# Recurrence scores level by level for a pair of head groups, with the projections' matmuls between the levels; six weight splits behind the norm chain; attention's first loads in another order

## The chip, the cores and the metric

The kernel runs on one core of one Trainium2 chip. The metric is the device time of one execution in microseconds (us). Engines are named as in the profile: PE is TensorE's matmul stream, PEld its weight loads, DVE is VectorE, ACT is ScalarE, SP issues the loads from HBM.

## What is computed

A two-layer network over 256 tokens of width 1024: a gated linear recurrence (HGRN2), a feed-forward block (FFN), sparse attention (NSA) with its shared keys and values, and a second FFN, each behind an RMS norm whose shift, scale and gate come from a conditioning vector c. The change touches the recurrence most:

```python
q, f, i, g = jnp.split(h @ w_in, ...)          # 8 heads, 128 keys and 128 values each
q = silu(q); log_f = log_sigmoid(f); k = -expm1(log_f)
# in chunks of 64 tokens, G = cumsum(log_f):
attn = einsum('bhtk,bhsk,bhtsk->bhts', q_, k_, decay)   # decay = exp(G_t - G_s), s <= t
o = attn @ v_ + (q_ * exp(G)) @ state
o = rms_norm(o, out_norm) * silu(g)
return o.reshape(B, S, HGRN_D_VAL) @ w_out
```

## The kernel before

The model's matrices arrive by DMA in tiles `raw` of 128 x 2048 floats. `process` (line 302) splits each half of such a tile into a high part `wh` (a cast on ACT, line 321) and a rest `wl` (a subtraction on DVE, line 325), and a product of the projections is three matmuls, wh by the high part of the activations, wh by their rest, wl by the high part (lines 529 to 531; for the values 972 to 974). DMA slots are few, so the next `raw` is issued when an earlier tile has been read for the last time. The conditioning is worked out by matmuls on the same PE (`adapsg`, `adapsss`, line 425, with transposes `adat`), sprinkled in by a table.

The recurrence handles the 8 heads as four groups i = 0 to 3 of two heads, and two groups make a pair. It does not run a scan. For every group it builds the 256 x 256 decayed score matrix from blocks by halving: `hgrn_decays` (line 994) holds running decays in `rf`, and for each level, with blocks of 1, 2, 4, 8, 16 and 32 tokens and more, writes a scaled copy of queries and keys, `X` (ACT, line 1023; DVE lines 1026 and 1028 carry `rf` to the next level). `hgrn_scores` (line 1033) then has PE multiply them. For each of four (head, token half) corners, `head_scores` issues 24 tiny matmuls into the tile `psl` (32-column diagonal blocks, line 1076, and five levels of 16 columns, line 1082) and 4 into `psu` (lines 1088, 1092); `psx` (line 1049) are the two large off-diagonal blocks. DVE masks `psl` into `ab` and then `A` (lines 1051 to 1062), ACT copies `psu` and `psx` in. `hgrn_values` multiplies A by the values v (`hgpv`, lines 1108 to 1110), normalises (`o`, line 1129), and transposes back (`hgt`, line 1132). The gate product g and the output projection `hgo` with its residual add `x` (line 794) follow.

The order of all this is the list ORDER["hgrn"], one token a step: D decays, i and g the value and gate products of a group, S a group's scores, V values, G gating, o output projection. A "+" puts a step's matmuls into a queue `between` instead, from which `hgrn_scores` draws `fill` steps of three matmuls after each corner (S0/4 draws four). S1 has no fill: its four corners, 96 tiny matmuls, follow each other. Every matmul on float32 data shows in the trace as two records.

`stat_end` (line 707) is the end of an RMS norm: `ms` on PE, a chain of small DVE operations from `nv` by three Newton steps (lines 488 to 493) to `dg`, and `rb` on PE (line 722), which spreads the result. On DVE's queue other work may stand between the links of this chain. ORDER["nsa"] and ORDER["hada"] place the attention's products and the conditioning in the same manner; PE, DVE and ACT each run their queue in program order.

Of the kernel before, what the change touches and what calls it, by code (L numbers as in the profile page):

```python
# [21 lines left out]
P = 128  # L22
# [8 lines left out]
XBUFS = 14  # L31
XMOD, XOFF = 5, 9
WIDE = (1,)
PTS = 3
# [20 lines left out]
def _ada_g(l):  # L55
# [9 lines left out]
        "D0 k i0 g0 S1 i1 +g1 S0/4 x c1 V0 D1 i2 i3 G0 +g2 +g3 +o0 S2/5 S3/5 V1 x H o1 G1 o2 o3"  # L65
# [4 lines left out]
        "c0 q0 c1 K G q1 n0 x0 s0 w0 q2 s1 q3 w1 s2 v0 v1 n1 s3 s4 a v2 v3 a a a x1 s5 a a s6 v4 v5 s7 a v6 a a "  # L70
        "a a v7 a"
# [128 lines left out]
class K:  # L200
# [101 lines left out]
    def process(self):  # L302
# [9 lines left out]
        if kind in ("lin", "half"):  # L312
            ws = []
            for h in range(1 if kind == "half" else 2):
# [10 lines left out]
                nc.vector.tensor_tensor(wl, u, wh.bitcast(F32), op=ALU.subtract)  # L325
# [88 lines left out]
    def ada_pe(self, kind, l, i, t):  # L414
# [19 lines left out]
        pt = self.m_tile([P, 4, P], "adat")  # L434
# [272 lines left out]
    def stat_end(self, ps=None):  # L707
# [11 lines left out]
        for tt in range(2):  # L719
            nc.vector.tensor_scalar_mul(dg[:, tt], self.c("ident"), r[:, tt:tt + 1])  # L720
# [93 lines left out]
    def hgrn(self):  # L814
# [3 lines left out]
        with self.tc.tile_pool(name="hg", bufs=1) as gp, self.tc.tile_pool(name="hg2", bufs=2) as g2:  # L818
# [19 lines left out]
            q = gp.tile([P, 8, S], F32, name="q")  # L838
# [8 lines left out]
            for i in range(4):  # L847
                self.act(q[:, 2 * i:2 * i + 2], pq[i], AF.Silu)
# [75 lines left out]
            Xs = {}  # L924
            for t in ORDER["hgrn"]:
# [3 lines left out]
                elif t[0] == "D":  # L929
                    Xs.update(self.hgrn_decays(logs if n == 0 else self.hgrn_logs({m: pf[m] for m in (2, 3)}, g2), q, g2))  # L930
                elif t[0] == "S":
                    As[n] = self.hgrn_scores(Xs.pop(n), q[:, 2 * n:2 * n + 2], g2, n, between, int(t[3:] or 0))
                elif t[0] == "+":
                    between = chain(between, {"g": gate_steps, "o": out_steps, "i": value_steps}[t[1]](int(t[2])))
# [11 lines left out]
                elif t[0] == "c":  # L946
                    nc.scalar.copy(graw[:, n], gin[n])
                elif t[0] == "V":
                    self.hgrn_values((2 * n, 2 * n + 1), As, v[n], g2, q)
# [44 lines left out]
    def hgrn_decays(self, logs, qs, g2):  # L994
# [16 lines left out]
        for i, rf in rfs.items():  # L1011
            nc.vector.tensor_tensor(rf[:, 0].rearrange("p (h s) -> p h s", h=2), rf[:, 2].rearrange("p (h s) -> p h s", h=2),
                                    qs[:, 2 * i:2 * i + 2], op=ALU.mult)
            nc.vector.tensor_copy(Xs[i][8], rf[:, 1].rearrange("p (h s) -> p h s", h=2))
        for l, b in enumerate(LEVELS):
            n = W // (2 * b)
            for i, rf in rfs.items():
                X = new(i, l)
                if b == 1:
                    odd = [[2, S]]  # L1020
                    nc.scalar.copy(ap(X, 1, *odd), ap(rf, 1, *odd))
                else:
                    last = nc.scalar.copy(ap(X, 0, [b, 2], [2 * b, n], [1, b]), ap(rf, W, [b - W, 2], [2 * b, n], [1, b]))  # L1023
# [9 lines left out]
    def hgrn_scores(self, X, q, g2, i, between, fill):  # L1033
# [3 lines left out]

        psl = self.m_tile([P, 4, 112], f"psl{i}")
        psu = self.m_tile([P, 4, P], f"psu{i}")
        psx = self.m_tile([P, 2, P], f"psx{i}")  # L1040
        for h in range(2):
            for tt in range(2):
                with self.tc.issue_after(prev.ins) if prev else ExitStack():
                    last = self.head_scores(psl, psu, X, q, h, tt)
# [4 lines left out]
            nc.tensor.matmul(psx[:, h], lhsT=X[7][:, h, 0:P], rhs=X[7][:, h, P:2 * P], start=True, stop=True)  # L1049
        ab = g2.tile([P, 4, 32], F32, tag="ab", name=f"ab{i}")  # L1050
        nc.vector.tensor_tensor(ab, psl[:, :, 0:32], self.c("m_d")[:, None, :].to_broadcast([P, 4, 32]), op=ALU.mult)
        ml = self.c("m_l").rearrange("p (l j) -> p l j", l=5)
        for l, b in enumerate(LOW):
# [3 lines left out]
            src = psl[:, :, 32 + 16 * l:48 + 16 * l].rearrange("p a (n b) -> p a n b", b=b)  # L1057
# [11 lines left out]
    def head_scores(self, psl, psu, X, q, h, tt):  # L1069

        nc = self.nc
        ht = h * 2 + tt
        base = tt * P
        for j in range(4):
            s = slice(base + 32 * j, base + 32 * j + 32)
            nc.tensor.matmul(psl[32 * j:32 * j + 32, ht, 0:32], lhsT=X[8][:, h, s], rhs=q[:, h, s],
                             start=True, stop=True, tile_position=(0, 32 * j))
        for l, b in enumerate(LOW):
            for j in range(4):
                s = slice(base + 32 * j, base + 32 * j + 32)  # L1080
# [10 lines left out]
        for j in (64, 0):  # L1091
            last = nc.tensor.matmul(u[j:j + 32, j + 32:j + 64], lhsT=X[5][:, h, base + j:base + j + 32],
                             rhs=X[5][:, h, base + j + 32:base + j + 64], start=True, stop=True,
                             tile_position=(0, j))
        return last

    def hgrn_values(self, ns, As, v, g2, q):
# [19 lines left out]
        else:  # L1117
# [8 lines left out]
            nc.vector.scalar_tensor_tensor(r, t, 1.5, r, op0=ALU.add, op1=ALU.mult)  # L1126
        for a, i in enumerate(ns):
# [540 lines left out]
```

## Time and profile before

| | |
|---|---|
| time, median of 3 runs | 734.29 us (733.88 to 738.5) |
| the profiled execution | 736.01 us, of which the span on the core is 734.2 us |
| TensorE clock granted, mean over the span | 0.998 |
| PE busy | 712.4 us (97%) |
| DVE busy | 580.3 us (79%) |
| ACT busy | 433.6 us (59%) |
| chain that ended last | PE 81%, ACT 7%, DVE 5%, DMA 4%, issue 1% |

The stages on PE's clock: conditioning and the input projections up to 72 us, the recurrence to 192 us, the first FFN to 365 us, keys and values and attention to 555 us, the second FFN to the end. A PE record in the trace lasts longer than its place in the stream, since matmuls are pipelined; the distance between two starts is what one costs.

### The profile page before, as it was taken

How to read it: one execution, taken by the hardware profiler on the slowest of the kernel's cores; microseconds unless marked ns; L12 is line 12 of the kernel's file. 1: busy time of each engine (PE TensorE's matmuls, PEld its weight loads, DVE VectorE, ACT ScalarE, POOL GpSimd, SP SyncE). 2: the span in 40 equal slices, each digit the busy share in tenths (PEclk: the TensorE clock that was granted, in tenths of full speed). 3: DMA queues.
4: the chain of work that ended last, by engine and by line, in shares of the span. 5: the costliest groups of instructions: out<-in, count | busy, mean ns of one | idle time of the engine just before them, and what ended most of it. 6: DMA issues, size and time to landing. Idle time of an engine off the chain costs nothing.

```text
span 734.2 us, 14785 instructions
## 1 busy us (share of the span) xinstructions
PE 712.4 (97%) x5949; PEld 626.6 (85%) x5949; DVE 580.3 (79%) x1177; ACT 433.6 (59%) x849; POOL 0.4 (0%) x5
## 2 busy tenths in 40 slices
PE   7999899999999999999999999999999999999997
PEld 4998688789999999988898897555899888888886
DVE  6997877469999889989589888678689778677651
ACT  5669689347635444534469777558666565655330
POOL 0000000000000000000000000000000000000000
PEclk9999999999999999999999999999999999999999
DMA  8899873823669897988555541654654557556610
GB/s 349 323 370 370 295 285 127 320 81 149 246 232 401 296 363 284 344 314 298 224 191 208 226 170 58 229 205 169 238 192 174 207 203 278 188 214 236 247 69 22
DMA packets 27159, 172.49 MB, mean 235 GB/s; under 512 B 2897, under 2 KB 4305, under 8 KB 7250
## 3 DMA queue, kind: packets, MB, share of 16 engines
q1 hardware_dynamic: 26656, 170.80, 62.7%
q8 instruction: 47, 0.77, 0.4%
q10 hardware_dynamic: 434, 0.74, 0.3%
q14 instruction: 22, 0.18, 0.1%
HBM read 170.48 MB, written 1.05 MB: 234 GB/s over the span
## 4 chain that ended last, share of the span: by engine, by line
PE 81%; ACT 7%; DVE 5%; DMA 4%; issue 1%; SPq 0%; ACTq 0%
PE ffo L541 11%; PE ff L530 6%; PE ff L529 6%; PE ff L531 6%; PE ffo L542 6%; PE ff L541 5%; DMA raw<-in_w 3%; PE po L1546 3%; PE ff L542 2%; PE adapsss L425 2%; ACT wh L321 2%; PE ptt L1529 2%; PE s L1489 2%; DVE wl L325 1%; PE nso L529 1%
## 5 line engine op out<-in xcount | busy, mean ns | idle before, releaser
L321 ACT CAST wh<-raw 128x1024 fp32r<-128x1024 f32 x199 | 207.4, 1048 | 170.2 <-PE ffo L541 48.6
L325 DVE TENSOR_TENSOR wl<-raw,wh 128x1024 fp32r<-128x1024 f32 x199 | 242.0, 1221 | 68.8 <-ACT wh L321 68.3
L541 PE MATMUL ffo<-g,wh 128*128 128x512 f32 x352 | 123.6, 394 | 0.0
L542 PE MATMUL ffo<-g,wl 128*128 128x256 f32 x352 | 99.1, 282 | 0.0
L531 PE MATMUL ff<-hh,wl 128*128 128x256 f32 (+1 forms) x352 | 99.1, 282 | 0.0
L530 PE MATMUL ff<-hl,wh 128*128 128x256 f32 (+1 forms) x352 | 98.8, 282 | 0.0
L529 PE MATMUL ff<-hh,wh 128*128 128x256 f32 (+1 forms) x352 | 98.6, 282 | 0.0
L541 PEld LDWEIGHTS ffo<-g,wh 128*128 128x128 f32 x352 | 66.1, 188 | 15.4
L387 DVE CUSTOM_DVE_ANT_0 junk<-raw,crep 128x1024 f32<-128x1024 f32 x64 | 77.9, 1218 | 1.8 <-DMA raw<-in_w 1.6
L531 PEld LDWEIGHTS ff<-hh,wl 128*128 128x128 f32 x352 | 66.5, 189 | 0.0
L530 PEld LDWEIGHTS ff<-hl,wh 128*128 128x128 f32 x352 | 66.3, 189 | 0.1
L529 PEld LDWEIGHTS ff<-hh,wh 128*128 128x128 f32 x352 | 66.1, 189 | 0.2 <-ACT hh L731 0.2
L542 PEld LDWEIGHTS ffo<-g,wl 128*128 128x128 f32 x352 | 66.1, 188 | 0.0
L541 PE MATMUL ff<-h,wh 128*128 128x512 f32 x152 | 54.0, 394 | 0.0
L542 PE MATMUL ff<-h,wl 128*128 128x256 f32 x152 | 42.6, 281 | 0.0
L541 PEld LDWEIGHTS ff<-h,wh 128*128 128x128 f32 x152 | 28.7, 189 | 6.5
L463 ACT ACTIVATE Pt<-Pt,nm 128x128 f32<-128x128 f32 x64 | 28.2, 442 | 8.1 <-DVE nm L1498 7.9
L794 DVE SCALAR_TENSOR_TENSOR x<-ffo,mod,x 128x256 f32<-128x256 f32 x32 | 15.4, 481 | 19.6 <-PE ffo L542 19.2
L542 PEld LDWEIGHTS ff<-h,wl 128*128 128x128 f32 x152 | 28.6, 188 | 0.0
L524 ACT CAST g<-fg 128x256 fp32r<-128x256 f32 x44 | 17.8, 404 | 14.1 <-DVE fg L1169 13.1
L1494 DVE CUSTOM_DVE_ANT_0 Pt<-s,cst 128x128 f32<-128x128 f32 (+1 forms) x64 | 19.0, 351 | 4.1 <-PE s L1489 4.1
L1026 DVE TENSOR_TENSOR rf<-rf 128x512 f32<-128x512 f32 x28 | 18.3, 685 | 2.8 <-ACT X L1023 1.8
(493 smaller groups left out, 1750.2 us busy)
## 6 DMA issues: line engine op xcount, KB each, us to landing
raw<-in_w SPq DMA_DIRECT2D x153, 1024.0 KB, 5.1
raw<-in_w SPq DMA_DIRECT2D x11, 512.0 KB, 6.6
w1late<-in_w SPq DMA_DIRECT2D x2, 1024.0 KB, 6.5
x<-in_x SPq DMA_DIRECT2D x2, 512.0 KB, 5.3
out<-x SPq DMA_DIRECT2D x8, 128.0 KB, 1.9
cst<-in_cst ACTq DMA_DIRECT2D x1, 558.0 KB
rselr<-in_rsel SPq DMA_DIRECT2D x1, 256.0 KB, 3.5
w<-in_w SPq DMA_DIRECT2D x1, 128.0 KB, 3.4
```

What stands on the lines that cost most here:

```text
L321: r = nc.scalar.copy(wh, u)
L325: nc.vector.tensor_tensor(wl, u, wh.bitcast(F32), op=ALU.subtract)
L387: r = nc.vector.tensor_tensor_reduce(out=junk, in0=t[:, h * D:(h + 1) * D], in1=self.crep, scale=1.0, scalar=0.0, op0=ALU.mult, op1=ALU.ad ...
L463: r = nc.scalar.activation(out, in_, func, **kw)
L529: mm(ps, lhsT=wh, rhs=hh, start=first, stop=False)
L530: mm(ps, lhsT=wh, rhs=hl, start=False, stop=False)
L531: return mm(ps, lhsT=wl, rhs=hh, start=False, stop=last)
L541: mm(ps, lhsT=w[k][0], rhs=b, start=k == 0, stop=False)
L542: mm(ps[:, 0], lhsT=w[k][1], rhs=b[:, 0], start=False, stop=k == n - 1)
L1026: nc.vector.tensor_tensor(fr, fr, ap(rf, 2 * W, [1, 2], [2, n], [0, b]), op=ALU.mult)
L1494: nc.vector.tensor_tensor_reduce(out=Pt[half][:, br, o:o + n], in0=ps[half][:, br], in1=cs[:, S - n:], scale=1.0, scalar=-3e38, op0=ALU.ad ...
L1546: nc.tensor.matmul(po[64 * half:64 * half + 64, t], lhsT=w[:, half], rhs=rhs, start=n == 0, stop=n == len(steps) - 1, tile_position=(0, 64 ...
```

## The change

It does five things.

1. Scores go by pair and by level: for a pair of groups the six levels are run one after the other, each as one slot of 16 matmuls per group, with `fill` steps of other work behind each slot; `psu` is the sixth level, and `psx` comes last in one tile of another PSUM tag. The masking is a function of its own, `hgrn_masks`, after all of them.
2. Level 0 is merged with the diagonal: the queries' tile `q` gets a third channel that holds the odd rows of `rf`, and one matmul of 48 columns does what one of 32 and one of 16 did. The level's `X` tile is gone (XBUFS 14 to 12), and everything that reads or writes `q` now does so with a stride of three floats.
3. The order: pair 0's fillers are g0, i1 and g1, pair 1's are i3, g2, T0 and g3. `hgrn_values` is cut in two, and its end (o, transposes, q) is a step of its own, T0 and T1. o0 and o1 move behind V1.
4. Six `wl` splits must come behind the last `dg` of their norm chain (ROOTED).
5. Attention's list starts with q0, q2 and q3 and two value steps swap, conditioning steps are spread singly; the `adat` tile moves to the PSUM tag "ada".

```diff
-XBUFS = 14
+XBUFS = 12
+ROOTED = [("ffn_in0", 2, 1), ("ffn_in0", 3, 0), ("kv", 2, 0), ("kv", 4, 0), ("ffn_in1", 2, 1), ("ffn_in1", 3, 0)]
...
-        "D0 k i0 g0 S1 i1 +g1 S0/4 x c1 V0 D1 i2 i3 G0 +g2 +g3 +o0 S2/5 S3/5 V1 x H o1 G1 o2 o3"
+        "D0 k i0 +g0 +i1 +g1 S0/4 x c0 c1 V0 D1 i2 +i3 +g2 +T0 +g3 S1/4 x G0 V1 T1 o0 H o1 G1 o2 o3"
...
-        "c0 q0 c1 K G q1 n0 x0 s0 w0 q2 s1 q3 w1 s2 v0 v1 n1 s3 s4 a v2 v3 a a a x1 s5 a a s6 v4 v5 s7 a v6 a a "
-        "a a v7 a"
+        "q0 c1 c0 K G q1 n0 x0 w0 s0 q3 s1 q2 w1 s2 v0 v1 n1 s3 a s4 v2 a v3 a x1 s5 a a s6 v4 v6 s7 v5 a v7 a a a a a a"
...
+                if (name, i, h) in ROOTED:
+                    self.after(r, self.last_dg)
...
-        pt = self.m_tile([P, 4, P], "adat")
+        pt = self.pp.tile([P, 4, P], F32, tag="ada", bufs=1, name="adat")
...
-            q = gp.tile([P, 8, S], F32, name="q")
+            q3 = gp.tile([P, 8, P, 3], F32, name="q")
+            q = q3[:, :, :, 0:2]
...
-                    As[n] = self.hgrn_scores(Xs.pop(n), q[:, 2 * n:2 * n + 2], g2, n, between, int(t[3:] or 0))
+                    As.update(self.hgrn_scores((2 * n, 2 * n + 1), Xs, q3, g2, between, int(t[3:] or 0)))
...
                 if b == 1:
-                    odd = [[2, S]]
-                    nc.scalar.copy(ap(X, 1, *odd), ap(rf, 1, *odd))
+                    odd = rf[:, 0].rearrange("p (h n two) -> p h n two", h=2, two=2)[:, :, :, 1]
+                    nc.scalar.copy(qs[:, 2 * i:2 * i + 2, :, 2], odd)
...
+    def hgrn_scores(self, pair, Xs, q3, g2, between, fill):
...
+        for l in range(6):
+            if l == 5:
+                psu = {i: self.m_tile([P, 4, P], f"psu{i}") for i in pair}
+            for i in pair:
+                q = q3[:, 2 * i:2 * i + 2]
                 with self.tc.issue_after(prev.ins) if prev else ExitStack():
-                    last = self.head_scores(psl, psu, X, q, h, tt)
+                    for ht in range(4):
+                        last = self.level_scores(l, psl[i], psu.get(i), Xs[i], q, ht)
                 with self.tc.issue_after(last.ins):
                     prev = None
                     for _ in range(fill):
                         prev = next(between, prev)
-            nc.tensor.matmul(psx[:, h], lhsT=X[7][:, h, 0:P], rhs=X[7][:, h, P:2 * P], start=True, stop=True)
+        psx = self.pp.tile([P, 4, P], F32, tag="acc", bufs=3, name=f"psx{pair[0]}")
...
+        for j in range(4 if l < 5 else 0):
             s = slice(base + 32 * j, base + 32 * j + 32)
...
+            if l:
...
+                r = q[:, h, base // 2 + 16 * j:base // 2 + 16 * j + 16].rearrange("p n c -> p (n c)")
+                lo, hi = 0, 48
+            last = nc.tensor.matmul(psl[32 * j:32 * j + 32, ht, lo:hi], lhsT=X[l or 8][:, h, s], rhs=r, start=True,
+                                    stop=True, tile_position=(0, 32 * j))
...
+    def values_end(self, ns, pvs, r, g2, q):
...
         for a, i in enumerate(ns):
             o = g2.tile([P, 4, P], F32, tag="o", bufs=1, name=f"o{i}")
...
+            yield last
```

Three places in the order of instructions. The first is PE at the start of the scores of the first pair. Before, behind the last gate product of group 0, group 1's corners stand in a row (the first two of four here):

```order
L531 MATMUL hg_g_967<-h_181,wl_1_877 128x256
L1076 MATMUL psl_1017<-q,X_8_777 32x32 x4
L1082 MATMUL psl_1017<-X_0_798,X_8_777 32x16 x4
L1082 MATMUL psl_1017<-X_1_806 32x16 x4
L1082 MATMUL psl_1017<-X_2_814 32x16 x4
L1082 MATMUL psl_1017<-X_3_822 32x16 x4
L1082 MATMUL psl_1017<-X_4_830 32x16 x4
L1076 MATMUL psl_1017<-q,X_8_777 32x32 x4
L1082 MATMUL psl_1017<-X_0_798,X_8_777 32x16 x4
L1082 MATMUL psl_1017<-X_1_806 32x16 x4
```

Now the first slot (group 0, level 0) stands ahead of the conditioning's `adapsg`, and between two slots stand twelve large matmuls:

```order
L985 MATMUL hg_i_848<-wh_1_763,h_181 128x256
L1108 MATMUL psl_929<-q,X_8_769 32x48 x16
L427 MATMUL adapsg_849<-raw_767,c_103 32x256 x8
L427 MATMUL adapsg_849<-raw_858,c_103 32x256 x8
L531 MATMUL hg_g_983<-h_181,wh_0_870 128x256
...
L533 MATMUL hg_g_983<-h_181,wl_0_871 128x256
L1108 MATMUL psl_930<-q,X_8_777 32x48 x16
L531 MATMUL hg_g_983<-h_181,wh_0_870 128x256
```

What moved: the 96 matmuls that stood together are spread over twelve slots, six of either group.

The second place is DVE in the second pair, where `o1`, which the transpose `hgt1` on PE needs, is computed. Before, with buffer numbers:

```order
L1129 TENSOR_TENSOR o0_1456<-hgpv0_1423,oy_1447 128x512
L325 TENSOR_TENSOR wl30_0_1608<-raw30_1255,wh30_0_1607 128x1024
L1129 TENSOR_TENSOR o1_1464<-hgpv1_1435,oy_1447 128x512
L325 TENSOR_TENSOR wl30_1_1612<-raw30_1255,wh30_1_1611 128x1024
L890 TENSOR_TENSOR g0_1666<-q_754,g0_1666 128x512
```

Now:

```order
L1037 TENSOR_TENSOR rf3_1430<-rf3_1430 128x2x4x64
L325 TENSOR_TENSOR wl33_0_1709<-raw33_1502,wh33_0_1708 128x1024
L325 TENSOR_TENSOR wl33_1_1713<-raw33_1502,wh33_1_1712 128x1024
L325 TENSOR_TENSOR wl36_0_1874<-raw36_1705,wh36_0_1873 128x1024
L1076 TENSOR_TENSOR ab2_1981<-psl2_1553,cst_80 128x128
L1160 TENSOR_TENSOR o1_1840<-hgpv1_1400,oy_1412 128x512
```

What moved: `o1` stood behind a split of tile 30 and stands now behind that of tile 36, the first tile of the output projection; the tile `o` has one buffer, so `o1` also waits for `hgt0`. On PE, `hgt0` and `hgt1` stand behind the first group's level 4, with matmuls of the conditioning between them.

The third place is DVE in the norm chain ahead of the first FFN. Before:

```order
L716 TENSOR_SCALAR nv<-ms 128x2
L325 TENSOR_TENSOR wl_1_2522<-raw_2227,wh_1_2521 128x1024
L488 TENSOR_SCALAR ny<-nv 128x2
L325 TENSOR_TENSOR wl_0_2624<-raw_2304,wh_0_2623 128x1024
L489 TENSOR_SCALAR ny<-ny 128x2
L325 TENSOR_TENSOR wl_0_2696<-raw_2390,wh_0_2695 128x1024
L491 TENSOR_TENSOR nt<-ny 128x2
L325 TENSOR_TENSOR wl_1_2628<-raw_2304,wh_1_2627 128x1024
L492 SCALAR_TENSOR_TENSOR nt<-nt,nv 128x2
```

Now:

```order
L718 TENSOR_SCALAR nv<-ms 128x2
L490 TENSOR_SCALAR ny<-nv 128x2
L491 TENSOR_SCALAR ny<-ny 128x2
L493 TENSOR_TENSOR nt<-ny 128x2
L494 SCALAR_TENSOR_TENSOR nt<-nt,nv 128x2
...
L722 TENSOR_SCALAR dg<-cst,ny 128x128 x2
L325 TENSOR_TENSOR wl_1_2452<-raw_2157,wh_1_2451 128x1024
L325 TENSOR_TENSOR wl_0_2554<-raw_2234,wh_0_2553 128x1024
```

What moved: the four splits that stood between the links stand behind `dg`. On PE, `ms` stands 29 matmuls behind the last `hgo` where it stood 39, and `rb` 29 behind `ms` where it stood 53.

## Rows read from the trace of the kernel before

**Rows 1.** The page: busy time of each engine, and the chain that ended last by line.

```profile
PE 712.4 (97%) x5949; PEld 626.6 (85%) x5949; DVE 580.3 (79%) x1177; ACT 433.6 (59%) x849; POOL 0.4 (0%) x5
...
PE 81%; ACT 7%; DVE 5%; DMA 4%; issue 1%; SPq 0%; ACTq 0%
```

**Rows 2.** The waits of PE over the whole span: total us, times, longest us.

```profile
PE psl L1082 <- issue: 3.7, 2, 3.0
...
PE rb L722 <- DVE dg L720: 1.9, 2, 1.3
```

**Rows 3.** PE's timeline in the first pair, 74 to 109 us: start, duration, engine, line, operation, operands, records, and in brackets the idle time ahead with what ended it. `hg_g` at 74.46 is the first gate product of group 0, `hg_i` at 108.85 the first value product of group 2.

```profile
74.46 0.39 PE L529 MATMUL hg_g<-h,wh 128*128 128x256 f32 x1
...
85.14 0.21 PE L1082 MATMUL psl<-X,X 128*32 128x16 f32 x3 [3.05 <-issue]
...
91.37 0.28 PE L972 MATMUL hg_i<-wh,h 128*128 128x256 f32 x1
...
96.58 0.28 PE L974 MATMUL hg_i<-wh,h 128*128 128x256 f32 x1
...
106.70 0.38 PE L1082 MATMUL psl<-X 128*32 128x16 f32 x24 [0.61 <-issue]
...
108.85 0.36 PE L972 MATMUL hg_i<-wh,h 128*128 128x256 f32 x1
```

**Rows 4.** [...]

```profile
82.10:85.10 3.00, 0.00 (x0) 0.00 (x0) 1.86 (x5) 0.33 (x1) 0.00 (x0) 1.00 0.65 221
85.60:89.10 3.50, 3.50 (x28) 1.25 (x24) 2.73 (x9) 3.50 (x7) 0.00 (x0) 0.53 0.57 185
```

**Rows 5.** PE's timeline in the second pair, 124 to 152 us: its first and last score matmuls, one 16-matmul run of the conditioning, the `psu` part of one slot, one undisturbed slot with the products around it, and the stall.

```profile
124.60 0.27 PE L1076 MATMUL psl<-q,X 128*32 128x32 f32 x8
...
135.79 1.93 PE L425 MATMUL adapsss<-raw,c 128*32 128x512 f32 x16
137.64 0.39 PE L529 MATMUL hg_g<-h,wh 128*128 128x256 f32 x1
...
140.69 0.25 PE L1088 MATMUL psu<-s 128*32 128x64 f32 x2
...
140.98 0.39 PE L529 MATMUL hg_g<-h,wh 128*128 128x256 f32 x1
...
142.77 0.28 PE L531 MATMUL hg_g<-h,wl 128*128 128x256 f32 x1
142.98 0.27 PE L1076 MATMUL psl<-q,X 128*32 128x32 f32 x8
...
143.51 0.22 PE L1092 MATMUL psu<-X 128*32 128x32 f32 x2
143.67 0.38 PE L529 MATMUL hg_g<-h,wh 128*128 128x256 f32 x1
143.89 0.28 PE L530 MATMUL hg_g<-h,wh 128*128 128x256 f32 x1
...
146.99 0.39 PE L531 MATMUL hg_g<-h,wl 128*128 128x256 f32 x1 [1.39 <-issue]
...
151.58 0.39 PE L1108 MATMUL hgpv<-v,A 128*128 128x128 f32 x2
```

**Rows 6.** ACT's timeline: two level copies of the first pair, in runs of two floats and of four.

```profile
70.89 1.29 ACT L1023 COPY X<-rf 128x512 f32<-128x512 f32 x2
...
72.99 1.15 ACT L1023 COPY X<-rf 128x512 f32<-128x512 f32 x2
```

**Rows 7.** DVE's timeline, 107 to 110 us: the first mask operation of group 0 and the one that ends its A.

```profile
107.16 0.29 DVE L1051 TENSOR_TENSOR ab<-psl,cst 128x128 f32<-128x128 f32 x1 [0.34 <-PE psl L1082]
...
109.90 0.69 DVE L1062 TENSOR_TENSOR A<-ab,cst 128x512 f32<-128x512 f32 x1
```

**Rows 8.** The timelines of SP, ACT and DVE around tile 36: the issue of its halves, the cast that waited for the first half, and the split behind it.

```profile
127.16 12.26 SPq L293 DMA_DIRECT2D raw<-in_w  x8
...
134.87 1.05 ACT L321 CAST wh<-raw 128x1024 fp32r<-128x1024 f32 x1 [5.47 <-DMA raw<-in_w]
...
135.95 1.23 DVE L325 TENSOR_TENSOR wl<-raw,wh 128x1024 fp32r<-128x1024 f32 x1 [4.94 <-ACT wh L321]
```

**Rows 9.** The norm chain ahead of the first FFN, DVE's timeline and then PE's: the chain's first and last operation, the last `hgo`, `ms`, `rb`.

```profile
184.48 0.15 DVE L716 TENSOR_SCALAR nv<-ms 128x2 f32<-128x2 f32 x1
...
191.60 0.48 DVE L720 TENSOR_SCALAR dg<-cst,ny 128x128 f32<-128x128 f32 x2
...
183.82 0.50 PE L713 MATMUL ms<-oneD,ssum 128*128 128x1 f32 x4
...
192.14 0.70 PE L722 MATMUL rb<-dg,ones 128*128 128x256 f32 x2 [1.34 <-DVE dg L720]
```

**Rows 10.** The norm chain ahead of keys and values, DVE's timeline: the chain's first operation, the one split that stands in it, and the end of the chain with what follows.

```profile
372.78 0.16 DVE L716 TENSOR_SCALAR nv<-ms 128x2 f32<-128x2 f32 x1 [0.72 <-PE ms L713]
...
374.31 1.22 DVE L325 TENSOR_TENSOR wl<-raw,wh 128x1024 fp32r<-128x1024 f32 x1 [0.37 <-ACT wh L321]
...
376.61 0.48 DVE L720 TENSOR_SCALAR dg<-cst,ny 128x128 f32<-128x128 f32 x2
377.01 1.22 DVE L325 TENSOR_TENSOR wl<-raw,wh 128x1024 fp32r<-128x1024 f32 x1
378.29 0.76 DVE L785 TENSOR_TENSOR u<-kv,rstd 128x256 f32<-128x256 f32 x2
```

More of the change, by code (lines that the diff above doesn't have):

```diff
@@ L923, in hgrn, with end_steps @@
             nxt = None
-            Xs = {}
+            Xs, ends = {}, {}
+            def end_steps(n):
+                yield from self.values_end(*ends[n])
             for t in ORDER["hgrn"]:
@@ L948, in hgrn @@
                 elif t[0] == "V":
-                    self.hgrn_values((2 * n, 2 * n + 1), As, v[n], g2, q)
+                    ends[n] = (2 * n, 2 * n + 1), *self.hgrn_values((2 * n, 2 * n + 1), As, v[n], g2, q), g2, q
+                elif t[0] == "T":
+                    for _ in self.values_end(*ends[n]):
+                        pass
                 elif t[0] == "G":
@@ L1031, in hgrn_decays @@
         return Xs
-    def hgrn_scores(self, X, q, g2, i, between, fill):
+    def hgrn_scores(self, pair, Xs, q3, g2, between, fill):
         nc = self.nc
         prev = None
[L1038 to L1042, printed above, removed]
+        psl = {i: self.m_tile([P, 4, 112], f"psl{i}") for i in pair}
+        psu, psx = {}, None
+        for l in range(6):
[3 more added lines that the diff above has]
+                q = q3[:, 2 * i:2 * i + 2]
                 with self.tc.issue_after(prev.ins) if prev else ExitStack():
-                    last = self.head_scores(psl, psu, X, q, h, tt)
+                    for ht in range(4):
+                        last = self.level_scores(l, psl[i], psu.get(i), Xs[i], q, ht)
                 with self.tc.issue_after(last.ins):
@@ L1048, in hgrn_scores, with hgrn_masks @@
                         prev = next(between, prev)
-            nc.tensor.matmul(psx[:, h], lhsT=X[7][:, h, 0:P], rhs=X[7][:, h, P:2 * P], start=True, stop=True)
+        psx = self.pp.tile([P, 4, P], F32, tag="acc", bufs=3, name=f"psx{pair[0]}")
+        with self.tc.issue_after(prev.ins) if prev else ExitStack():
+            for i in pair:
+                for h in range(2):
+                    X = Xs[i][7][:, h]
+                    nc.tensor.matmul(psx[:, 2 * (i - pair[0]) + h], lhsT=X[:, 0:P], rhs=X[:, P:2 * P], start=True, stop=True)
+        return {i: self.hgrn_masks(psl[i], psu[i], psx[:, 2 * (i - pair[0]):2 * (i - pair[0]) + 2], g2, i) for i in pair}
+    def hgrn_masks(self, psl, psu, psx, g2, i):
+        nc = self.nc
         ab = g2.tile([P, 4, 32], F32, tag="ab", name=f"ab{i}")
-        nc.vector.tensor_tensor(ab, psl[:, :, 0:32], self.c("m_d")[:, None, :].to_broadcast([P, 4, 32]), op=ALU.mult)
+        qk = psl[:, :, 0:48].rearrange("p a (n c) -> p a n c", c=3)
+        md = self.c("m_d").rearrange("p (n two) -> p n two", two=2)[:, None].to_broadcast([P, 4, 16, 2])
+        nc.vector.tensor_tensor(ab.rearrange("p a (n two) -> p a n two", two=2), qk[:, :, :, 0:2], md, op=ALU.mult)
         ml = self.c("m_l").rearrange("p (l j) -> p l j", l=5)
```

49 lines of the change are left out of this document (24 added, 25 removed).

## The prediction

> **What bounds the kernel now.** I read the page first: PE is busy 97% of the span, and the chain that ended last runs on PE for 81% of it [rows 1]. So a change gains by what it takes out of PE's stream: idle time, matmuls, or the clock. The waits of PE come next [rows 2]. The largest that the change touches are two "issue" waits of 3.7 us ahead of `psl`, a third "issue" wait of 1.39 us ahead of `hg_g` [rows 5], and 1.9 us ahead of `rb`. The timeline then shows where they stand. The 3.05 us stall comes in the middle of S1, where tiny matmuls follow each other with nothing between them [rows 3]; the 0.61 us one is inside a filled slot [rows 3], the 1.39 us one behind a filled slot [rows 5]. [...] The stages behind the recurrence have no such idle time, so I work out the recurrence piece by piece and treat the rest as small corrections.
>
> **Prices on PE.** A 256-column product costs 0.118 us (44 starts from 91.37 to 96.58) [rows 3]. A run of 16 conditioning records costs 1.85 us [rows 5]. An undisturbed slot of 56 tiny records: the products on either side start 0.90 us apart instead of 0.12, and the second product behind it comes 0.10 us late too (0.22 instead of 0.12) [rows 5]. So a slot costs 0.88 us. Its records start over 0.53 us, 0.0096 us each, so entering and leaving cost 0.34 us whatever stands inside [rows 5]. A new slot has 32 records of 16 columns: 0.34 + 32 x 0.0096 = 0.65 us. Level 0 has 48 columns, for which there is no row; below it lies the price of 16 and 32 columns (0.65 us), above it twice that per record (0.96 us). I take 0.76, nearer the lower end, since the 32-column records in the undisturbed slot are no slower. `psu` matmuls: the eight of one slot take 0.29 us up to the next product [rows 5], of which 0.16 is leaving, so 0.016 to 0.023 each; I take 0.02, and a slot of 32 costs 0.98 us. The joined `psx` (8 records of 128 columns, 0.06 us each at half a 256-column product) with its 0.34 comes to 0.8 us.
>
> **Pair 0.** Before: 34.4 us from the first gate product to the first value product of group 2 [rows 3]. In it are 144 products (17.0 us), two runs of the conditioning (3.7 us) and a transpose (0.2 us), so the scores with all that they bring cost 13.5 us: 3.7 us stalls, some 1.7 us clock (3.5 us at 0.53) [rows 4], 8.1 us work. After: group 0's level 0 moves into the wait for a weight tile that precedes this stretch and costs nothing; were that tile early, it would cost 0.76. What remains is one level-0 slot, eight plain, two `psu` and `psx`: 0.76 + 5.2 + 1.96 + 0.8 = 8.7 us. Gain 4.8 us (3.5 to 6). Merging level 0 takes out 128 records in both pairs, 1.2 us, and the added slots' entering and leaving give it back; both are in this sum.
>
> **Pair 1.** Before: 27.0 us from 124.60 to 151.58 [rows 5], less 108 products (12.8), two runs (3.7) and a transpose (0.4): 10.1 us. After: 2 x 0.76 + 5.2 + 1.96 + 0.8 = 9.5 us. Gain 0.6 us (-0.5 to 1.7). The 1.39 us stall goes, more entering comes.
>
> **New waits.** V0 reads A1 at once where value products of group 2 stood ahead. From the first mask to the end of A, DVE took 3.4 us for a group, mixed with `rf` work [rows 7]. From group 0's first mask to A1's end its queue now holds twice that, two splits of 1.2 us [rows 8] and six more operations of D1 (0.6 each, as the last of the masks [rows 7]), together 12.8 us. The mask can start when group 0's level 4 is through, which is, counted back on PE from a first value product at 102.7 (108.85 less most of the gain and with a `hgpv` matmul ahead), 11 us earlier, at about 92. So A1 is whole at 104.8 and ACT's copies of `psu` end some 0.7 us later; PE wants A1 at 104.8. -0.7 us (0 to 1.5). In pair 1, `o1` stands on DVE behind the split of tile 36. Before, the tile was issued at 127.16, 0.15 us behind the conditioning run that freed its slot, its cast started 7.7 us later and its split 1.1 us after that [rows 8]; nothing on PE needed DVE then. Now with split (1.1), first mask (0.2) and `o1` (0.7) the transpose could start 0.15 + 7.7 + 1.1 + 2.0 = 11.0 us after that run; PE gets there after 48 products (5.7), four more slots (2.6), `hgt0` and ten conditioning records (1.5), that is 9.8 us. -1.2 us (0 to 2.5, as the tile lands). What queues behind `hgt1` on PE is g3, and behind `o1` on DVE are the gating of pair 0 and the masks of pair 1, which have g3 as cover.
>
> **Output stage.** o0 and o1 behind V1 give the DVE chain of V1 (o, transposes, gating) 78 products as cover instead of about 57. The two short waits for x there are under 1 us; I take +0.4 us (-1 to +0.8).
>
> **Norm chains.** Ahead of the first FFN four splits stood in a chain of 7.5 us from `nv` to the end of `dg` [rows 9]. The chain at keys and values shows its own length: 4.2 us from `nv` to the end of `dg`, less a split of 1.1 and a wait of 0.37 [rows 10], 2.8 us. But PE's order uses that up: `ms` comes 39 - 29 = 10 products earlier and `rb` 24 earlier still, 4.0 us. `ms` to `rb` needs 0.5 + 2.8 + 0.3 = 3.6 us against 29 products = 3.4 us, and `ms` waits for the last sums on DVE, which three splits still precede. So 0.9 us of the 1.34 us wait remains: gain 0.4 us (0 to 1.3). At keys and values the chain gets 1.5 us shorter and `rb` moves up, yet two splits (2.4 us) then stand ahead of `u`, where one stood [rows 10]; gain 0.3 us (0 to 0.6). At the second FFN PE hardly waits: nothing. Attention's reordering moves loads and steps that PE does not wait for: 0 (-0.7 to +0.7); its cover is the conditioning steps, now spread thinner.
>
> [...] q is now written and read with a stride of three floats. Where the profile has copies in runs of two floats and of four, 512 elements cost 0.64 and 0.57 us [rows 6], so 0.07 us per operation at most, and of some 16 operations on q hardly one is on PE's path: nothing in my sum. [...] No run here shows a stride of three yet.
>
> **Sum.** +4.8 + 0.6 - 0.7 - 1.2 + 0.4 + 0.4 + 0.3 = 4.6 us. The profiled execution took 736.01 us, so 731.4; it lies 1.7 us above the median of the three runs, 734.29 us, against which I predict 729.7 us.
>
> **Rivals.**
> (a) *The stalls' gain is given back at once* (chance 0.20). Waits at their upper ends (V0 1.5, `hgt1` 2.5), pair 1 -0.5, x -1.0, norm chains 0: 4.8 - 5.5 = -0.7, so 735 us; half of that, 732 to 733 us. For it: DVE is 79% busy [rows 1] and now carries both pairs' masks in one lump. Against: gate products g2, g3 and o0 stand as cover.
> (b) *No new wait shows* (chance 0.20). The loads start earlier because PE runs earlier, tile 36 lands in time, and `rb` waits no more: 4.8 + 0.6 + 0.8 + 1.3 + 0.6 = 8.1 us, 726.2 us. For it: landing times of loads spread by microseconds. Against: the DVE queue is in program order, so A1 and `o1` move only as the queue does.
> (c) *The slots themselves stall* (chance 0.10). The 0.61 us and 1.39 us stalls were in or behind filled slots [rows 3, 5], so filling alone does not exclude them. There are now 24 slots; at 0.61 each that is 14.6 us, less the sum 4.6: 10 us slower, 744 us. It turns the sign at 4.6 / 24 = 0.19 us per slot. Against: a slot has 32 records instead of 56 with as many products behind it, and only two of the eight filled slots of pair 1 stalled by more than a trace.
> (d) *PE doesn't gain where it stopped idling* (chance 0.05): the clock falls in another place, at a wait of `hgt1` as long as the 3 us one was; 3 + 1.7 us lost, 733 to 734 us.
>
> **How the numbers follow.** My own forecast, 726 to 732 us, has 0.45. The range 724.5 to 735.5 us takes in (a) and (b) and leaves out most of (c) and the far ends of the bounds, about 2 in 10. Faster by over 1% means under 726.9 us: (b) and the near end of my own case, 0.29. Slower by over 1% means above 741.6 us: (c), 0.09. Within 1%, 0.62. About one per cent is what a measurement of this kernel can tell from no change.
>
> **What would show each step.** In the profile of the changed kernel: no "issue" wait over 0.3 us ahead of `psl` or `hg_g`, and the clock at 1.00 from 85 to 90 us; the first value product of group 2 near 103 us instead of 108.85; products on either side of a slot 0.7 us apart; a wait of `hgpv` for A near 105 us and of `hgt` for `o` near 130 us, each about 1 us; `rb` near 187 us with a wait under 1 us. Wrong would be: "issue" waits in the slots (c), waits of `hgpv` or `hgt` over 2 us (a), none at all (b), or a slot that costs over 1 us.

## The result, and the profile after

The changed kernel takes 726.84 us (median of 4 runs, 725.66 to 728.47) beside 734.09 us before on the same chip: a ratio of 0.990 (95% interval 0.986 to 0.994), 7.25 us less. A later comparison on another occasion gave 726.33 beside 734.29 us, a ratio of 0.9893 (0.9872 to 0.9915). The forecast was 4.6 us less, to 729.7 us: the result lies in the predicted range, at the near end of the forecast's own interval (726 to 732 us), and closest to rival (b), 726.2 us.

The page of the changed kernel, the lines that answer to [rows 1]; its span is 724.7 us, 9.5 us less than that of before, of which 0.7 us were gained before the recurrence begins, ahead of everything that the change touches there. The profiled execution of before took 736.01 us, 1.9 us over the median, so the differences between the two profiles below add up to more than the 7.25 us between the medians:

```profile
PE 711.4 (98%) x5821; PEld 626.3 (86%) x5821; DVE 578.6 (80%) x1177; ACT 433.7 (60%) x849; POOL 0.4 (0%) x5
...
PE 84%; ACT 7%; DVE 6%; DMA 2%; issue 1%; ACTq 0%
```

PE's waits from 60 to 200 us, recurrence and first norm, in the changed kernel: the view lists one, where [rows 2] had "issue" waits and `rb`. Under it, the two stretches of [rows 4], where PE now never stops and the clock stays up (in a line of windows: busy us and records of PE, PEld, DVE, ACT and POOL, PE's granted clock as a share of its full speed, the DMA engines' share, GB/s):

```profile
PE hg_g L533 <- DVE wl L325: 0.6, 1, 0.6
```

```profile
82.10:85.10 3.00, 3.00 (x34) 1.61 (x26) 2.27 (x6) 2.76 (x6) 0.00 (x0) 1.00 0.87 303
85.60:89.10 3.50, 3.50 (x86) 3.31 (x86) 2.45 (x2) 3.47 (x6) 0.00 (x0) 1.00 0.99 368
```

To see where the time went, I read PE's timeline at places that both kernels have (`hg_i` are the value products of the recurrence, `ffo` the second product of an FFN, `kv` keys and values, `s` the attention's scores), and took the differences of the starts. This table carries the comparison of all runs below (us, one profiled execution each):

| kernel | first `hg_i` | from there to the first `ffo` (recurrence, norm, first half of FFN 0) | first `kv` to first `s` (keys, values, queries) | first `s` to PE's last start |
|---|---|---|---|---|
| before | 63.57 | 243.49 | 78.01 | 283.15 |
| changed | 62.83 | 234.84 | 77.68 | 283.37 |
| changed, again | 62.18 | 234.70 | 77.66 | 283.33 |

The first column spreads over 1.39 us in these three executions, by 0.65 us in the two of the changed kernel; the others repeat within 0.15 us for the changed one. So the change gains 8.7 us in the second column and 0.3 in the third and loses 0.2 in the fourth. Within the second, the changed kernel's distance ahead of before grows by 5.0 us up to the first value product of group 2 (108.85 before, 103.11 now, less the 0.74 of the start), by 0.3 us more up to V1 (both counted without the `hgo` that stood ahead of it), 1.4 us in the output stage and 1.9 us at the norm.

PE's timeline of the changed kernel, a level-0 slot and a plain one in pair 1, with the product on either side:

```profile
111.69 0.28 PE L985 MATMUL hg_i<-wh,h 128*128 128x256 f32 x1
111.90 0.55 PE L1108 MATMUL psl<-q,X 128*32 128x48 f32 x32
112.38 0.39 PE L983 MATMUL hg_i<-wh,h 128*128 128x256 f32 x1
...
115.87 0.28 PE L985 MATMUL hg_i<-wh,h 128*128 128x256 f32 x1
116.08 0.45 PE L1108 MATMUL psl<-X 128*32 128x16 f32 x32
116.46 0.39 PE L983 MATMUL hg_i<-wh,h 128*128 128x256 f32 x1
116.68 0.28 PE L984 MATMUL hg_i<-wl,h 128*128 128x256 f32 x1
```

The products on either side of a plain slot start 0.59 us apart and the next follows 0.22 us later: 0.57 us for a slot as the prediction counts it (it had 0.65), 0.67 for a level-0 slot (0.76).

The transpose `hgt1` in the changed kernel, on PE, DVE and ACT (cast, split, first mask, `o1`, transpose), where [rows 8] had nobody waiting behind the cast:

```profile
130.80 1.90 PE L427 MATMUL adapsss<-raw,c 128*32 128x512 f32 x10
132.78 0.65 PE L1163 MATMUL hgt<-cst,o 128*128 128x128 f32 x4
```

```profile
130.70 1.23 DVE L325 TENSOR_TENSOR wl<-raw,wh 128x1024 fp32r<-128x1024 f32 x1 [6.83 <-ACT wh L321]
131.84 0.28 DVE L1076 TENSOR_TENSOR ab<-psl,cst 128x128 f32<-128x128 f32 x1
132.04 0.68 DVE L1160 TENSOR_TENSOR o<-hgpv,oy 128x512 f32<-128x512 f32 x1
```

```profile
129.62 1.05 ACT L321 CAST wh<-raw 128x1024 fp32r<-128x1024 f32 x1 [5.95 <-DMA raw<-in_w]
```

The chain is the one that was foreseen: `o1` ends at 132.72 us and `hgt1` starts at 132.78. But PE hardly waits for it. Ten `adapsss` records take 1.98 us by starts here, and in the second profile of the changed kernel, where `o1` was whole 0.11 us ahead of `hgt1`, they take 1.84 us (PE, then DVE):

```profile
130.13 1.90 PE L427 MATMUL adapsss<-raw,c 128*32 128x512 f32 x10
131.97 0.66 PE L1163 MATMUL hgt<-cst,o 128*128 128x128 f32 x4
131.18 0.68 DVE L1160 TENSOR_TENSOR o<-hgpv,oy 128x512 f32<-128x512 f32 x1
```

So the wait is some 0.14 us. What costs PE time is that `hgt1` splits a run of the conditioning: ten records cost as much as sixteen (1.85 us, 135.79 to 137.64 in [rows 5]), and the six behind `hgt1` cost 0.98 us more:

```profile
133.37 1.06 PE L427 MATMUL adapsss<-raw,c 128*32 128x512 f32 x6
134.35 0.39 PE L531 MATMUL hg_g<-h,wh 128*128 128x256 f32 x1
```

The split run costs 2.82 us instead of 1.85, that is 0.97 us, which is not in the prediction's sum. (Two expectations below have a wait of 0.66 us for `hgt1`: it came from a price of 1.3 us for ten records.)

The norm ahead of the first FFN in the changed kernel, PE's timeline (last `hgo`, `ms`, `rb`) and DVE's (last split ahead of the chain, the chain's ends), beside [rows 9]:

```profile
172.58 0.28 PE L533 MATMUL hgo<-hh,wl 128*128 128x256 f32 x1
176.19 0.50 PE L715 MATMUL ms<-oneD,ssum 128*128 128x1 f32 x4
180.11 0.60 PE L724 MATMUL rb<-dg,ones 128*128 128x256 f32 x2
```

```profile
175.88 1.22 DVE L325 TENSOR_TENSOR wl<-raw,wh 128x1024 fp32r<-128x1024 f32 x1
177.01 0.15 DVE L718 TENSOR_SCALAR nv<-ms 128x2 f32<-128x2 f32 x1
...
179.37 0.48 DVE L722 TENSOR_SCALAR dg<-cst,ny 128x128 f32<-128x128 f32 x2
```

The last `dg` ends at 179.85 us, 0.26 us before PE comes to `rb`; neither `ms` nor `rb` waits.

### The profile page after: what moved, and what is told of

Read it like the earlier page. It is cut to its first block, busy times and chain, and to the rows that moved or that the text cites. A ratio compares the mean times of both kernels' runs of the same rounds, so it can differ in the third digit from the quotient of the medians.

```text
span 724.7 us, 14519 instructions
## 1 busy us (share of the span) xinstructions
PE 711.4 (98%) x5821; PEld 626.3 (86%) x5821; DVE 578.6 (80%) x1177; ACT 433.7 (60%) x849; POOL 0.4 (0%) x5
## 4 chain that ended last, share of the span: by engine, by line
PE 84%; ACT 7%; DVE 6%; DMA 2%; issue 1%; ACTq 0%
PE ffo L543 11%; PE ff L531 6%; PE ff L533 6%; PE ff L532 6%; PE ffo L544 6%; PE ff L543 5%; PE po L1578 3%; PE ff L544 2%; PE adapsss L427 2%; PE ptt L1561 2%; PE s L1521 1%; PE nso L531 1%; ACT wh L321 1%; PE nso L533 1%; PE cmp L1416 1%; PE hg_g L531 1%
```

## The experiments

In S1 of the kernel before, 112 tiny matmuls of group 1 follow each other (96 into `psl` and 16 into `psu`); they now stand in six of pair 0's twelve slots.

Theory: the long "issue" waits come from unbroken stretches of tiny matmuls, and the change gains most by breaking them up (with the clock that a stall costs); the ROOTED list gives the rest. Rivals: the stalls belong to their place in the program; the merge of level 0 does it; the list gives little, as the prediction had it.

**Unfilled slots.** Pair 0's order is "D0 k i0 g0 i1 +g1 S0 x c1 V0": all the slots stand behind i1 with nothing between them.

```diff
-        "D0 k i0 +g0 +i1 +g1 S0/4 x c0 c1 V0 ...
+        "D0 k i0 g0 i1 +g1 S0 x c1 V0 ...
```

> The changed kernel with pair 0's slots unfilled: g0 and i1 first, then the level slots of pair 0 in a row, then g1. Levels, merge and all else stay. Theory (an unbroken run of some 250 tiny records empties what PE has to issue, as in S1 of the kernel before): an issue wait of 2 to 3.5 us inside psl, the clock near 0.5 for some 3 us behind it, together 4 to 6 us more than the changed kernel, and up to 5 us more where V0 now waits for A. Rival (the stall of before belonged to its place and its loads, not to the run): no issue wait over 0.5 us, and only V0's wait, 0 to 5 us.

Measured: 730.99 us, ratio 0.9967 (0.9947 to 0.9988); second column 238.67, 3.9 us more than the changed kernel. PE's timeline shows the stalls again, at another place and with other instructions than before, and windows the clock behind them:

```profile
92.64 1.12 PE L1108 MATMUL psl<-X 128*32 128x16 f32 x101 [3.07 <-issue]
96.09 0.27 PE L1114 MATMUL psu<-s 128*32 128x64 f32 x1 [1.19 <-issue]
```

```profile
89.50:92.60 3.10, 0.07 (x8) 0.00 (x0) 0.69 (x1) 1.49 (x3) 0.00 (x0) 1.00 1.02 381
93.00:96.00 3.00, 1.91 (x107) 1.67 (x96) 2.47 (x13) 0.00 (x0) 0.00 (x0) 0.56 0.05 16
96.00:99.50 3.50, 3.41 (x46) 3.25 (x45) 1.39 (x3) 0.00 (x0) 0.00 (x0) 0.50 0.03 7
```

So the stall goes with the unbroken run, not with S1's place. V0 did not wait. By an estimate from these rows, the two stalls (4.3 us) and the low clock (6.8 us at 0.50, so up to 3.4 us; in the corner kernel below, products start 0.21 us apart at 0.50 and 0.12 us at 1.00) cost up to 7.7 us; that the kernel loses only 3.9 fits that it enters and leaves eleven slots less (some 0.3 us each). The DMA view gives a hint at what PE waits for, and no more: in the kernel before, one packet of the instruction queue (q8) arrives within the stall of [rows 3]. The DMA view from 82.7 to 83.7 us, queue, packets, MB:

```profile
q1 hardware_dynamic: 29, 0.15, 40.8%
q8 instruction: 1, 0.02, 5.8%
```

In the unfilled kernel too there is one such packet between 88 and 92.7 us, while the loads keep the DMA engines full (share 1.02 above). But the changed kernel also has one from 80 to 85 us, where PE does not stop:

```profile
q8 instruction: 1, 0.02, 1.3%
```

And the DMA engines are nearly idle (share 0.05) from 93 to 96 us, where the unfilled kernel's second stall falls. That the instructions themselves came late is possible; no run here changes that supply alone, so it is not shown.

**Half the filler.** g0 stands ahead, and the slots of pair 0 have six products between them.

```diff
-        "D0 k i0 +g0 +i1 +g1 S0/4 x c0 c1 V0 ...
+        "D0 k i0 g0 +i1 +g1 S0/2 x c1 V0 ...
```

> The changed kernel with g0 ahead of the scores and pair 0's slots filled by six products instead of twelve (i1 and half of g1). Theory (slots of 32 records with 0.7 us of products between them are loose enough): no issue wait over 0.3 us, a slot costs 0.60 us as in the changed kernel, and the time is within 1 us of it, V0's wait for A (up to 1 us) aside. Rival (it is the records per microsecond that count): issue waits of 0.3 to 0.6 us in several slots, 1.5 to 4 us more.

Measured: 727.86 us, ratio 0.9925 (0.9898 to 0.9952); second column 235.91, 1.1 us more. Between theory and rival: all slots run clean but one, ahead of which PE waits. In PE's timeline:

```profile
90.81 0.28 PE L985 MATMUL hg_i<-wh,h 128*128 128x256 f32 x1
92.04 0.45 PE L1108 MATMUL psl<-X 128*32 128x16 f32 x32 [0.95 <-issue]
```

**Corners, filled.** The kernel before with its corner-by-corner scores; S1 stands behind i1, and the eight corners of pair 0 have six products each.

```diff
-        "D0 k i0 g0 S1 i1 +g1 S0/4 x c1 V0 ...
+        "D0 k i0 g0 i1 +g1 S1/2 S0/2 x c1 V0 ...
```

> The kernel before with its own corner-by-corner scores, but S1 behind i1 and the eight corners of pair 0 filled by six products of g1 each. Theory (the long stall is from the missing filler; 56 records per 6 products still outrun the supply in places): the 3.05 us wait is replaced by issue waits of 0.3 to 0.8 us in some corners, 1 to 2.5 us in all, the clock stays at 1.00, and the time is 2 to 4.5 us under before, so filling explains most of pair 0's gain. Rival (the order by level is what it takes): stalls of 2 us or more again, within 1.5 us of before.

Measured: 740.23 us, ratio 1.0096 (1.0066 to 1.0126): slower than before, so my expectation fell. The profiled execution is the slowest of the seven (744.25 us). PE's timeline and a window:

```profile
94.50 0.18 PE L1082 MATMUL psl<-X,X 128*32 128x16 f32 x1 [0.30 <-issue]
...
100.43 0.57 PE L1082 MATMUL psl<-X 128*32 128x16 f32 x29 [2.19 <-issue]
```

```profile
100.10:110.30 10.20, 9.87 (x178) 8.75 (x178) 4.44 (x11) 3.05 (x7) 0.00 (x0) 0.50 0.05 18
```

The lower clock comes with a 2.19 us stall here and stays for 10.2 us, with PE busy nearly all along. Not all of the loss is from these stalls: `hgt` then waits 2.7 us for `o`, where it did not wait before, and the mean granted clock over the span of 742.4 us is 0.986, by an estimate from these figures some 10 us more at 0.50 than the window shows. Some filler is not enough: 56 records with six products between them stall, 32 with six stall once, 32 with twelve not at all. Nor is much filler behind long slots: S0, S2 and S3 of the kernel before had 56 records per twelve or fifteen products, and showed a stall of 0.61 us [rows 3] and one of 1.39 us [rows 5]. Running by level makes the slots short and, by the two lists, lets the first of them start when level 0 alone is ready, so that pair 0's scores are spread over g0, i1 and g1 (144 products) instead of g1 alone (48). No run keeps the corners and gives all eight of them twelve products.

**Without the ROOTED list.** The changed kernel with the list empty.

```diff
-ROOTED = [("ffn_in0", 2, 1), ...]
+ROOTED = []
```

> The changed kernel with an empty ROOTED list: the four splits stand between the links of the norm chain ahead of the first FFN again, and rb stands 54 products behind ms instead of 29. Theory (the list is worth what rb no longer waits): the chain takes some 7.5 us again against 54 products = 6.4 us, so rb waits 1.0 to 1.5 us and the kernel takes 1.0 to 1.9 us more than the changed one, about 728 to 728.7 us. Rival (the gain at the norm chain comes from the output projections' new place): rb waits under 0.4 us and the time is within 0.5 us of the changed kernel.

Measured: 729.18 us, ratio 0.9927 (0.9901 to 0.9953); second column 236.65 (1.8 us more), third 78.00 (0.3 more). PE's waits:

```profile
PE rb L724 <- DVE dg L722: 1.8, 2, 1.3
```

The 1.3 us wait is back, as the theory has it.

**The list alone.** The kernel before with the list and the three lines that use it, and no more.

> The kernel before with the ROOTED list alone. Theory: rb's wait of 1.34 us goes, since the chain is 2.8 us and 30 products (3.6 us) stand between ms and rb: 1.3 to 1.9 us less than before, about 732.5 us. Rival (the prediction's own working: ms comes too late for it): 0.3 to 0.6 us less.

Measured: 731.16 us, ratio 0.9953 (0.9935 to 0.9972). More than the theory, but the profile says why: second column 238.58, 4.9 us less than before, of which its distance ahead grows by 1.9 us at the norm. The rest is the execution, since pair 0 is unedited: its stalls happened to be shorter (`psl` 3.0 us in place of 3.7, `hg_g` 0.5 in place of 1.4), and the clock did not fall. PE's timeline, and the window behind the stall:

```profile
82.85 0.21 PE L1085 MATMUL psl<-X,X 128*32 128x16 f32 x3 [2.18 <-issue]
```

```profile
82.90:86.40 3.50, 3.50 (x85) 1.52 (x85) 2.38 (x7) 3.26 (x7) 0.00 (x0) 1.00 0.89 314
```

So a stall of 2.2 us can cost the clock, as in the corners above, or not, as here. From the first value product of the recurrence to that of group 2 this kernel takes 42.81 us, before 45.28 and the changed kernel 40.28: what the change gains in pair 0 is 5.0 us against one execution and 2.5 against the other. The times show it too. Before took 731.15 to 738.05 us in 17 runs; the five of them with a mean granted clock of 1.000 took 731.15 to 733.28, the three with 0.993 or 0.994 took 736.99 to 738.05. The changed kernel took 725.66 to 728.47 in 10.

**Level 0 unmerged.** Each 48-column matmul as one of 32 and one of 16 columns.

```diff
+                nc.tensor.matmul(psl[32 * j:32 * j + 32, ht, 0:32], lhsT=X[8][:, h, s], rhs=r[:, 0:32], ...)
+                r, lo = r[:, 32:48], 32
```

> The changed kernel with each 48-column level-0 matmul issued as one of 32 and one of 16 columns from the same tile: 64 matmuls (128 records) more, nothing else. Theory (a tiny record costs about 0.0096 us whatever its width): 0.8 to 1.3 us more than the changed kernel. Rival (width decides, so that 48 columns cost what 32 and 16 do): within 0.4 us.

Measured: 726.75 us, ratio 0.99 (0.9878 to 0.9923): the times cannot tell the two kernels apart. The profile can. A level-0 slot of pair 1 in its timeline, first and last product:

```profile
112.58 0.28 PE L985 MATMUL hg_i<-wh,h 128*128 128x256 f32 x1
...
113.55 0.39 PE L983 MATMUL hg_i<-wh,h 128*128 128x256 f32 x1
```

0.97 us instead of 0.69, so 32 more records cost 0.28 us, 0.009 each. Pair 0 loses 1.25 us by it (two slots, and 0.6 us of "issue" waits that come back). Pair 1 loses next to nothing: its two slots cost 0.56 us more, but V0, to which PE comes later, takes 3.65 us in place of 4.04, and `hgt1` no longer waits (0.14). The second column is 236.18, 1.3 us more. The merge is worth about 1 us in the profile, too little for the times to show, and not what makes the gain.

**T0 late, T0 early.** The transposes behind g3, and ahead of g2, in place of ahead of g3.

```diff
-+g2 +T0 +g3 S1/4
++g2 +g3 +T0 S1/4      (late)
++T0 +g2 +g3 S1/4      (early)
```

> The changed kernel with T0 behind g3 instead of behind g2, so that hgt0 and hgt1 stand behind all slots of pair 1. Theory (hgt1 waits 0.66 us for o1, which waits for tile 36): that wait goes, 0.3 to 0.7 us less. Rival (the transposes' end is needed early by the gating): the first hgo waits for the gated values, 0.5 to 2 us more.

> The changed kernel with T0 ahead of g2, so that in DVE's order o1 stands behind the split of tile 33 instead of that of tile 36. Theory (hgt1 waits 0.66 us since o1 stands behind a split whose tile lands late): hgt1's wait goes or shrinks to 0.2 us, 0.3 to 0.7 us less than the changed kernel. Rival (any place of T0 waits for o, which has one buffer and follows the last decays on DVE): a wait of 0.6 us or more for o0 or o1 in the new place, no gain.

Late: 727.45 us, ratio 0.9919 (0.9894 to 0.9945), second column 235.85, 1.0 us more. Both views fell: the conditioning run stays whole, but PE waits in the transposes themselves, which now follow each other; `o` has one buffer, so `o1` is made only when `hgt0` is done:

```profile
PE hgt L1163 <- DVE o L1160: 1.7, 1, 1.7
```

Early: 726.47 us beside 726.33 of the changed kernel on the same chip. `hgt1` does not wait, as the theory says, and yet the second column is 234.95 beside 234.70. There was no wait of 0.66 us to take out: the transposes split a conditioning run here as well, into two and fourteen records, which cost 0.97 and 1.84 us, as much as the ten and six:

```profile
120.24 1.04 PE L427 MATMUL adapsss<-raw,c 128*32 128x512 f32 x2
121.21 0.66 PE L1163 MATMUL hgt<-cst,o 128*128 128x128 f32 x4
121.80 1.92 PE L427 MATMUL adapsss<-raw,c 128*32 128x512 f32 x14
123.64 0.39 PE L531 MATMUL hg_g<-h,wh 128*128 128x256 f32 x1
```

An order in which the run stays whole and `o1` is ready in time was not run; by these rows it would be worth up to 1 us.

**The attention's list and adat's tag.** Old list with the new tag; old list and old tag; new list with the old tag.

> The changed kernel with the attention's list of before. Theory (the new list moves loads and steps that PE does not wait for): within 0.5 us of the changed kernel. Rival (the earlier query load or the spread conditioning matters): 0.7 us or more to one side, with other waits of nq, hs or s.

> The changed kernel with both the attention's list and the PSUM tag of adat as before. With the old list alone the stretch from the first s to the second FFN's fourth product took 120.4 us in the profile, where the changed kernel has 117.6 and the kernel before 117.4. Theory (the old list holds the tile that adat now shares with the conditioning's sums, and the new list undoes that): the stretch is back at 117.3 to 117.8 us and the kernel within 0.5 us of the changed one. Rival (the old list itself is slower beside the other changes, or that profile was an odd one): 119.5 us or more, or 117.5 us with no cause.

> The changed kernel with only adat's PSUM tag as before. Theory (list and tag together give nothing by themselves): the stretch at 116.8 to 117.8 us, the kernel within 0.7 us of the changed one. Rival (the new list needs the new tag, or is worth something alone): over 1 us to either side.

| list, tag | time, us | ratio (interval) | first `s` to the end |
|---|---|---|---|
| new, new (changed, again) | 726.33 | 0.9893 (0.9872 to 0.9915) | 283.33 |
| old, new | 728.02 | 0.9916 (0.9894 to 0.9938) | 285.43 |
| old, old | 726.07 | 0.9875 (0.9846 to 0.9904) | 283.16 |
| new, old | 725.73 | 0.9878 (0.9842 to 0.9914) | 282.73 |

The first expectation fell: the old list with the new tag is 1.2 to 1.7 us slower than the changed kernel. The other two held, beside the 726.33 us of the changed kernel. In the profile, one execution each, the new tag costs 2.3 us with the old list and 0.6 us with the new; the list without the tag gains 0.4 us. Together, as the change has them, they give nothing, as forecast. The times point the same way, with overlapping intervals. (My measure in two of the expectations, up to the second FFN's fourth product, mixes in where that product stands; the table's goes to PE's last start.) The two kernels with the old tag are the fastest of the study by median, but not clear of the changed one.

## Why the prediction was right, and where its sizes were off

The range held because it was drawn wide enough to take in rival (b). The sum was not as good: 4.6 us, against 7.25 us between the medians and 9.5 us from the profile of before, whose rows it was added up from, to that of the changed kernel.

- *What bounds it*: right. The gain is PE time: idle time, and the clock behind it.
- *Pair 0, +4.8*: 5.0 measured, by the way that was named: no "issue" wait, clock at 1.00 where it was at 0.53 [rows 4], the first value product of group 2 at 103.11 us. The unfilled kernel brings the stalls and the low clock back. The size is in part luck: the fall of the clock is one execution's, and in the list-alone kernel, where it did not come, the changed kernel's lead over the same stretch is 2.5 us.
- *Prices of a slot*: 0.57 and 0.67 us against 0.65 and 0.76, a little too dear. The forecast that dropped records cost 0.0096 us each is borne out by the unmerged kernel (0.009).
- *V0's wait, -0.7*: 0.3 us by starts. PE lost 0.23 us at 104.15 us behind ACT's copy of `psx` into A0, and 0.04 at 105.65 behind A1's last copy, which ended at 105.60 us, as worked out (105.5); but PE came to it 0.8 us later than I had it.
- *hgt1's wait, -1.2*: the chain was right, the size was 0.14 us. The cast came 7.3 us behind the issue in place of 7.7, and PE came 10.4 us behind the conditioning run in place of 9.8: `hgt0` and ten records, which I had at 1.5 us by the price of one record in sixteen, cost 2.4 us. The split of the run, 0.97 us, I had put at nothing without seeing it.
- *Pair 1, +0.6 with V0 -0.7 and hgt1 -1.2*: +0.3 in all. The ten cheaper slots give some 0.8 us more than I had, the split takes 1.0.
- *Output stage, +0.4*: 1.4 measured. The two waits for `x` counted 0.39 and 0.82 us by starts, and both are gone; I had counted on a third of that. No run takes out the new place of o0 and o1 alone, so that it is the cause is argued and not shown.
- *Norm ahead of the FFN, +0.4*: 1.9 measured. This is the term that was most mis-sized. The chain's own length (2.8 us) was right, but I let `ms` wait for the last sums, and it did not: the last `ssum` ended on DVE at 175.96 us, and PE came to `ms` at 176.19. The third split stands behind that sum and held up only `nv`. I also set the chain's 3.6 us against 29 products alone (3.4 us), and left out the time of `ms` itself on PE: from `ms` to `rb` PE took 3.92 us. The list alone gives 1.9 us here in the kernel before, and taking it out of the changed one brings 1.8 us back, so the gain is the list's. (The sign "`rb` near 187 us" left out what the recurrence gains ahead of it; it ran at 180.11.)
- *Keys and values, +0.3; attention, 0; second FFN, 0*: 0.3, -0.2 and nothing.
- *The stride of three floats, nothing in the sum*: no wait of PE shows it, though one copy is slower by more than I allowed. Operations on `q` before (first two rows) and after (last two), as nanoseconds min, median, max:

```profile
L463 ACT ACTIVATE q<-q x4: 593/602/620, 67.4 to 68.8; 128x512 f32<-128x512 f32 x4
L890 DVE TENSOR_TENSOR g<-q,g x4: 678/688/693, 126.0 to 165.5; 128x512 f32<-128x512 f32 x4
```

```profile
L465 ACT ACTIVATE q<-q x4: 609/624/644, 66.6 to 68.1; 128x512 f32<-128x512 f32 x4
L894 DVE TENSOR_TENSOR g<-q,g x4: 683/684/684, 133.9 to 155.1; 128x512 f32<-128x512 f32 x4
```

These operations touch two floats of every three and cost ACT 0.02 us more each and DVE nothing that shows. What writes only every third float is the copy of the odd rows into the third channel, 256 elements; before, the same copy wrote every second float of `X` (first row):

```profile
L1021 ACT COPY X<-rf x4: 426/442/472, 69.3 to 102.5; 128x256 f32<-128x256 f32 x4
L1031 ACT COPY q<-rf x4: 540/551/559, 68.6 to 97.2; 128x256 f32<-128x256 f32 x4
```

It is 0.11 us slower, a quarter, which is more than the 0.07 us that I allowed. From 60 to 200 us PE's one wait in the view is for a split (0.6 us, above); none is put down to these copies.

Nearly all the misses have one sign: the new waits that I charged came smaller, and of the old ones I kept, none was left. That is what rival (b), 726.2 us, said. The split of the conditioning run is the miss of the other sign. Rival (c), slots that stall, is refuted for twelve products per slot, but not far off: with six there is one stall of 0.95 us, and with 56 records per six products the kernel is slower than before.

## What to carry to other kernels

Tiny matmuls are not only their own time: spread them, with enough large products between them (here twelve between 32 records; with six there was a stall of 0.95 us), and price a slot by entering and leaving (here about 0.3 us) as well as by its records (0.009 us each). A stall of PE costs its own length, and more where the clock falls behind it (to 0.50 for 3.4 us behind one of 3.05 us, not at all behind one of 2.18); read the granted clock in the window behind each long wait, and in more than one execution, before you count on that part. When you move an operation into a run of others, read what the pieces of the run cost: here ten records cost what sixteen do. A chain of tiny DVE operations that PE waits for should have no long work between its links (four splits there cost 1.8 us here), but ask what the postponed work then stands in front of.

## What the runs showed of the hardware

"Issue" waits of PE of 1 to 3 us went with how many tiny matmuls stand together, and with the execution: 249 `psl` records in a row stalled for 3.07 us, 32 between six products once for 0.95 us, 32 between twelve not at all; the same unedited scores stalled for 3.05 us in one profile and for 2.18 in another. Behind stalls of 3.05 and 3.07 us the granted clock was at 0.50 for some 3.4 and 6.8 us (a stall of 1.19 us stands in the latter), behind one of 2.19 us for 10.2 us, with PE busy by the records; behind one of 2.18 us it stayed at 1.00. A run of 16 `adapsss` records cost 1.85 us and pieces of it of ten or fourteen cost 1.84, pieces of two or six 0.97 or 0.98. On ACT, a copy of 256 floats took 551 ns when it wrote every third float, 442 when it wrote every second; with two of every three floats used, 512 took 624 ns beside 602 packed, and DVE 684 beside 688.
